# Tokens as the stationary operand: turning the products of a two-network kernel round

## The chip, the cores and the metric

The kernel runs as one program on one core of a Trainium2 chip. Its metric is device time in microseconds (us) of one execution; the time given for a kernel is the median of its runs. TensorE (PE) multiplies, VectorE (DVE), ScalarE (ACT) and GpSimd (POOL) do the work between products, and SyncE (SP) issues most loads.

## The reference, cut to what matters

The input x has 256 tokens of 1024 features. It passes through two networks of two layers each. Every layer is a feed-forward block, a mixer and a second feed-forward block, each added to the residual:

```python
def swiglu(h, w_in, w_out):
    gate, up = jnp.split(h @ w_in, 2, axis=-1)      # w_in (1024, 2 * 2816)
    return (jax.nn.silu(gate) * up) @ w_out         # w_out (2816, 1024)

def rmsnorm(x, g):
    return x * lax.rsqrt(jnp.mean(x * x, axis=-1, keepdims=True) + EPS) * g

x = x + 0.5 * swiglu(rmsnorm(x, g0), w_in0, w_out0)
x = x + mixer(rmsnorm(x, g1), ...)
x = x + 0.5 * swiglu(rmsnorm(x, g2), w_in1, w_out1)
```

The mixers are, in order: hgrn2 (`hg`: a gated linear recurrence with 8 heads, weights 1024 x 4096 and 1024 x 1024), forgetting attention (`fox`: 16 heads, the same sizes and 16 more columns), a short convolution (`conv`: 1024 x 3072 and 1024 x 1024), and a sparse attention with three branches (`nsa`), whose shared keys and values (`kv`: 1024 x 1536) are projected once from the residual ahead of the last layer. All of it is fp32.

## The kernel before

Thirteen phases run one after the other: ffn 0, hg 1, ffn 2, ffn 3, fox 4, ffn 5, ffn 6, conv 7, ffn 8, kv 9, ffn 10, nsa 11, ffn 12. The residual `x` stays on the chip with features on partitions: 8 tiles of 128 features by 256 tokens.

Each product of fp32 numbers is made of three: both operands are split into a rounded part and a rest, both in the type fp32r, and hi x hi, hi x lo and lo x hi are added in PSUM. `mm_w` multiplies with the weights stationary (128 x 128) and 256 tokens moving, and gives an output with features on partitions; `mm_x` has 128 tokens stationary and 256 weight columns moving.

```python
self.mm(out, h[:, k, s], xh[:, k], start, False, 109.0)
self.mm(out, h[:, k, s], xl[:, k], False, False, 109.0)
self.mm(out, l[:, k, s], xh[:, k], False, stop, 109.0)
```

The weights come in pieces of 1 MB, 336 in all: an `in` piece is 1024 rows by 256 columns, an `out` piece 256 rows by 1024 columns. `load` brings a piece to a raw buffer (`wr`, 4 of them), `prep` splits a quarter of it: ScalarE casts the high part `wh` (L177) and VectorE subtracts to get the low part `wl` (L179), or GpSimd does so for the quarters named in `pool_parts`. There are 4 pairs of split buffers. The order of everything is written out by hand: `self.t` counts modelled time along the products, `pump` emits a quarter of a split every `pace` ns if buffers allow, and `tick` lets background tasks (`spawn`) emit their next part when it is due. Each engine runs its own instructions in the order in which they were emitted.

A feed-forward unit (11 per block) takes a gate piece and an up piece of 256 columns: `proj` makes 2 x 16 products of three matmuls into two PSUM banks. `g1` is the gate times 1/rms, spread over partitions as `rb` (L477, VectorE), `sg` its silu (L479, ScalarE) times 1/rms again (L480, GpSimd), `av` the up half times `sg` (L484), and `ah`, `al` are its parts (L487, L488). `proj_out` multiplies the unit before with its `out` piece, 16 products, into four banks that add up over the block.

`leave` and `enter` join blocks: as a pair of output tiles is complete, VectorE adds it to `x` (L392), ScalarE and VectorE split x times the norm's gain into `xh`, `xl` (L356, L360), ScalarE squares (L370) and GpSimd adds the squares up (L372, L382). `stats` sums them over partitions with narrow matmuls (`consts,ssum`), takes the inverse root on VectorE in small steps (`rsqrt`), and `spread` puts 1/rms on all partitions with two matmuls (`dg,consts`). The first unit of a block goes through k in its outer loop, so that it can start on the first tiles of x.

In fox, kv and nsa, `nat_heads` norms heads of q and k with tokens on partitions: square (L674), sum (L675), `rsqrt`, and the factor applied as `qn` (L686), which also frees the PSUM bank; `turn` and `to_feature` transpose 128 x 128 blocks on TensorE (L250).

Of the kernel before, what the change touches and what calls it, by code (L numbers as in the profile page):

```python
# [8 lines left out]
F32 = mybir.dt.float32  # L9
# [14 lines left out]
FAR = 1e30  # L24
LEVELS = (1, 2, 4, 8, 16, 32, 64)
# [18 lines left out]
# columns of the array of per-partition vectors  # L44
# [9 lines left out]
# columns of the array of row vectors, the same on each partition  # L54
# [3 lines left out]
# columns of the array of constants  # L58
# [8 lines left out]
def positions():  # L67
    """NSA: the head at position 2 * c + half, chunk c = 4 * pair + hg."""
    return [(2 * (c // 4) + half) * 4 + c % 4 for c in range(8) for half in range(2)]


def plan(phases=PHASES):
    """The weight pieces in the order of their use: (array, index, 'in'|'out', columns or rows)."""
# [8 lines left out]

    for ph in phases:
        if ph[0] == "ffn":
            _, _, w_in, at, w_out = ph
            for u in range(NU):
                pieces.append((w_in, at, "in", block(u)))
                pieces.append((w_in, at, "in", block(NU + u)))
                if u:
                    pieces.append((w_out, at, "out", block(u - 1)))  # L90
            pieces.append((w_out, at, "out", block(NU - 1)))
        elif ph[0] == "hg":
            for p in range(4):
                pieces += [("hg_w_in", (0,), "in", block(4 * s + p)) for s in range(3)]
            pieces += [("hg_w_in", (0,), "in", block(12 + p)) for p in range(4)]
            pieces += [("hg_w_out", (0,), "out", block(p)) for p in range(4)]
        elif ph[0] == "fox":
            pieces += [("fox_w_in", (0,), "in", block(0)), ("fox_w_in", (0,), "in", block(4))]
            pieces.append(("fox_w_in", (0,), "in", range(4096, 4112)))
            pieces.append(("fox_w_in", (0,), "in", block(8)))  # L100
            for p in range(1, 4):
                pieces += [("fox_w_in", (0,), "in", block(4 * s + p)) for s in range(3)]
            pieces += [("fox_w_in", (0,), "in", block(12 + p)) for p in range(4)]
            pieces += [("fox_w_out", (0,), "out", block(p)) for p in range(4)]
        elif ph[0] == "conv":
            for p in range(4):
                pieces += [("conv_w_in_2", (0,), "in", block(4 * s + p)) for s in range(3)]
# [1472 lines left out]
```

## Time and profile before

| what | us |
|---|---|
| time, median of 3 runs (2153.5 to 2154.3) | 2153.77 |
| span of the profiled execution, first to last instruction | 2149.8 |
| busy: TensorE, weight loads, VectorE, ScalarE, GpSimd | 2097.8, 2072.7, 1409.2, 1034.0, 432.4 |
| feed-forward block 2, windows 386 to 577.6 | 191.6 |
| hg, 202.6 to 386 | 183.4 |
| fox, 768.1 to 934.2 | 166.1 |

The span is what one profiled execution shows; its own time is known only through the runs, whose median lies 4.0 us above the span, outside the first and last instruction. PE is the matmuls, whose records overlap since they are pipelined, PEld the weight loads. PEclk is the granted clock of TensorE as a share of full speed (1.00 is 2.4 GHz, 0.50 is 1.2 GHz). Each matmul record is named output<-moving,stationary. An fp32 product that is not fp32r is two instructions in the trace, a transpose is one.

### The profile page before, as it was taken

What the parts mean: (1) busy time and instruction counts of PE and PEld (TensorE: products, weight loads), DVE (VectorE), ACT (ScalarE), POOL (GpSimd) and SP (SyncE); (2) the same over time, 40 slices, a digit from 0 to 9 for tenths busy, and PEclk for the clock granted to TensorE, in tenths of its full rate; (3) what the DMA queues carried; (4) which work ended last, traced back from release to release, by engine and by line L of the source; (5) the groups of instructions that cost most, each with busy time, mean ns of one, the idle gap of its engine ahead of it and who ended that gap; (6) DMA issues with size and microseconds to landing.
All of it is one profiled execution on the core that took longest, in us unless ns stands there. A gap on an engine that the chain in (4) does not pass through costs nothing.

```text
span 2149.8 us, 41509 instructions
## 1 busy us (share of the span) xinstructions
PE 2097.8 (98%) x17273; PEld 2072.7 (96%) x17273; DVE 1409.2 (66%) x2536; ACT 1034.0 (48%) x2082; POOL 432.4 (20%) x410
## 2 busy tenths in 40 slices
PE   8999889999999997999999999999999999999999
PEld 8999889999999997999999999999999999889999
DVE  7666676755665576466567567776578665677654
ACT  5544434444454456654444444454445444665442
POOL 2002546300100026420011001110021100532000
PEclk9999999999999999999999999999999999999999
DMA  7554423595455534345545554555546555223551
GB/s 263 203 189 146 154 80 128 178 239 189 157 212 183 184 141 165 128 143 213 194 157 196 181 192 141 202 194 191 180 169 234 179 185 174 101 94 120 213 193 60
DMA packets 56701, 367.88 MB, mean 171 GB/s; under 512 B 6255, under 2 KB 10631, under 8 KB 13761
## 3 DMA queue, kind: packets, MB, share of 16 engines
q1 hardware_dynamic: 53600, 355.49, 46.2%
q0 software_dynamic: 2336, 9.02, 2.2%
q8 instruction: 135, 2.21, 0.4%
q10 hardware_dynamic: 576, 0.72, 0.1%
q14 instruction: 54, 0.43, 0.1%
HBM read 359.70 MB, written 4.46 MB: 169 GB/s over the span
## 4 chain that ended last, share of the span: by engine, by line
PE 73%; DVE 7%; ACT 2%; issue 1%; POOL 0%; DMA 0%; DVEq 0%; ACTq 0%
PE b L245 72%; DVE wl L179 2%; DVE xl L360 1%; PE b L250 1%; DVE x L392 1%; ACT wh L177 1%; DVE rs_t L423 1%; DVE rs_t L424 0%; ACT xh L356 0%; DMA cd<-cn 0%; DVE oc L1260 0%; DVE rn L425 0%; DVE nrs L425 0%; POOL ssum L372 0%; DVE nss L675 0%
## 5 line engine op out<-in xcount | busy, mean ns | idle before, releaser
L179 DVE TENSOR_TENSOR wl<-wr,wh 128x512 fp32r<-128x512 f32 x1229 | 849.6, 750 | 256.7 <-ACT wh L177 256.4
L245 PE MATMUL b<-xh,wh 128*128 128x256 f32 x3184 | 908.0, 285 | 7.0 <-ACT wh L1442 7.0
L245 PE MATMUL b<-xh,wl 128*128 128x256 f32 x3184 | 904.7, 284 | 2.5 <-DVE wl L1443 2.5
L245 PE MATMUL b<-xl,wh 128*128 128x256 f32 x3184 | 904.1, 284 | 0.0
L177 ACT CAST wh<-wr 128x512 fp32r<-128x512 f32 x1332 | 725.9, 616 | 149.9 <-issue 132.1
L245 PEld LDWEIGHTS b<-xh,wh 128*128 128x128 f32 x3184 | 613.5, 193 | 7.1 <-ACT wh L1442 7.0
L245 PEld LDWEIGHTS b<-xh,wl 128*128 128x128 f32 x3184 | 613.5, 193 | 3.4 <-DVE wl L1443 3.4
L245 PEld LDWEIGHTS b<-xl,wh 128*128 128x128 f32 x3184 | 613.6, 193 | 0.0
L245 PE MATMUL b<-ah,wh 128*128 128x256 f32 x1408 | 394.4, 280 | 0.0
L245 PE MATMUL b<-al,wh 128*128 128x256 f32 x1408 | 394.2, 280 | 0.0
L245 PE MATMUL b<-ah,wl 128*128 128x256 f32 x1408 | 394.0, 280 | 0.0
L480 POOL TENSOR_TENSOR sg<-sg,rb 128x512 f32<-128x512 f32 x88 | 114.3, 1298 | 1247.5 <-ACT sg L479 1247.5
L245 PEld LDWEIGHTS b<-al,wh 128*128 128x128 f32 x1408 | 265.1, 188 | 0.2 <-DVE al L488 0.2
L245 PEld LDWEIGHTS b<-ah,wh 128*128 128x128 f32 x1408 | 265.1, 188 | 0.0
L245 PEld LDWEIGHTS b<-ah,wl 128*128 128x128 f32 x1408 | 264.7, 188 | 0.0
L479 ACT ACTIVATE sg<-g 128x512 f32<-128x512 f32 x88 | 55.6, 632 | 320.5 <-DVE g L477 320.4
L487 ACT CAST ah<-av 128x512 fp32r<-128x512 f32 x88 | 54.6, 621 | 259.1 <-DVE av L484 259.1
L477 DVE TENSOR_TENSOR g<-b,rb 128x512 f32<-128x512 f32 x88 | 60.7, 690 | 170.9 <-PE b L245 169.0
L179 POOL TENSOR_TENSOR wl<-wr,wh 128x512 fp32r<-128x512 f32 x103 | 143.1, 1402 | 132.6 <-ACT wh L177 126.2
L245 PE MATMUL b<-wh,xh 128*128 128x256 f32 x512 | 152.7, 298 | 11.5 <-DVE qn L686 11.5
L245 PE MATMUL b<-wl,xh 128*128 128x256 f32 x512 | 146.5, 286 | 0.0
L245 PE MATMUL b<-wh,xl 128*128 128x256 f32 x512 | 146.4, 286 | 0.0
(264 smaller groups left out, 1970.9 us busy)
## 6 DMA issues: line engine op xcount, KB each, us to landing
wr<-in_W_dram SPq DMA_DIRECT2D x332, 1024.0 KB, 4.8
td<-t POOLq DMA_DIRECT2D x1, 3072.0 KB, 37.9
wr<-in_W_dram SPq DMA_DIRECT2D x8, 256.0 KB, 6.1
bc<-cd POOLq DMA_DIRECT2D x4, 512.0 KB, 5.2
w<-in_CW_dram POOLq DMA_DIRECT2D x2, 1024.0 KB, 10.3
bt<-td SPq DMA_DIRECT2D x8, 256.0 KB, 3.9
x<-in_XT_dram SPq DMA_DIRECT2D x4, 256.0 KB, 5.9
wr<-in_W_dram SPq DMA_DIRECT2D x2, 512.0 KB, 3.8
```

What stands on the lines that cost most here:

```text
L177: nc.scalar.copy(h[:, s], r[:, s])
L179: eng.tensor_tensor(l[:, s], r[:, s], h[:, s].bitcast(F32), op=ALU.subtract)
L245: self.nc.tensor.matmul(out, lhsT, rhs, start=start, stop=stop, skip_group_check=True)
L250: self.nc.tensor.transpose(out, in_, self.c("ID")[:n, :n])
L360: self.nc.vector.scalar_tensor_tensor(xs[1][:, d], self.x[:, d], g, xs[0][:, d].bitcast(F32), op0=ALU.mult, op1=ALU.subtract)
L392: nc.vector.scalar_tensor_tensor(x, acc[i], factor, x, op0=ALU.mult, op1=ALU.add)
L423: nc.vector.scalar_tensor_tensor(t, out, -1.0, out, op0=ALU.mult, op1=ALU.mult)
L477: nc.vector.tensor_tensor(g1, banks[0].rearrange("p (c t) -> p c t", c=2), self.rb2(), op=ALU.mult)
L479: nc.scalar.activation(sg, g1, AF.Silu)
L480: nc.gpsimd.tensor_tensor(sg, sg, self.rb2(), op=ALU.mult)
L487: nc.scalar.copy(ah, av)
```

## The change

The order of operands is turned in most products. Tokens (128 at a time) are stationary and weights move, 512 columns at once. This takes pieces of another shape: an `in` unit is now two half pieces, each 512 rows by 512 columns (for a feed-forward unit, 256 gate and 256 up columns side by side), `out` pieces stay as they were. `nat` makes one bank of 128 tokens by 512 columns from 8 products; `out_steps` makes the residual's increment by tokens. Only products whose result must have features on partitions (q and the forget gate of hg, all of conv, the compressed keys and values of kv, the narrow projections `mini`) keep the old order, in `feat` and `mini`.

The residual is kept by tokens, 2 tiles of 128 tokens by 1024, and `enter` turns a quarter of it (4 transposes), splits it into `xs`, and takes the sum of squares along the free axis on ScalarE. 1/rms is then a scalar per partition, so a feed-forward unit needs no `rb`: silu takes it as its scale, and `av` is one multiply with two factors. `av` has tokens on partitions and is turned (4 transposes) by the task `turn`, due 2000 ns after the unit's products, and split by `to_feature`. Only hg, conv and kv still call `spread`. The norm's gain leaves the residual's split and enters that of `in` pieces, as a scale on ScalarE and a multiply-subtract on VectorE; these pieces no longer go to GpSimd. Raw buffers are 3 instead of 4, `consts` is loaded ahead of `vec`, and input and output are laid out by tokens. In fox the ring of banks for projections has 3 banks from the start, q and k of four heads share one `nat_heads`, and `mini` and the first half of v come behind it; in kv the normed keys are made first, then `spread`, then the raw keys and values.

```diff
 def plan
+    def cols(name, at, site, idx):
+        for half in range(2):
+            pieces.append((name, at, "in", list(idx), half, site))
...
-                pieces.append((w_in, at, "in", block(u)))
-                pieces.append((w_in, at, "in", block(NU + u)))
+                cols(w_in, at, site, [*block(u), *block(NU + u)])
...
-        self.wraw = pool("wraw", 4)
+        self.wraw = pool("wraw", 3)
 def prep
-        nc.scalar.copy(h[:, s], r[:, s])
-        eng = nc.gpsimd if self.part in self.pool_parts else nc.vector
-        eng.tensor_tensor(l[:, s], r[:, s], h[:, s].bitcast(F32), op=ALU.subtract)
+        if kind == "in":
+            g = self.gain(site, 4 * half + q)
+            nc.scalar.activation(h[:, s], r[:, s], AF.Copy, scale=g)
+            nc.vector.scalar_tensor_tensor(l[:, s], r[:, s], g, h[:, s].bitcast(F32), op0=ALU.mult, op1=ALU.subtract)
+        else:
...
+            nc.scalar.copy(h[:, s], r[:, s])
+            eng = nc.gpsimd if q in self.pool_parts else nc.vector
+            eng.tensor_tensor(l[:, s], r[:, s], h[:, s].bitcast(F32), op=ALU.subtract)
...
+    def three(self, out, a, b, start, stop, cost):
+        (ah, al), (bh, bl) = a, b
+        self.mm(out, ah, bh, start, False, cost)
+        self.mm(out, ah, bl, False, False, cost)
+        self.mm(out, al, bh, False, stop, cost)
...
+    def nat_steps(self, w, j, b):
+        self.finish(*self.entering[:2 + 2 * j])
         s = slice(128 * j, 128 * j + 128)
+        for k in range(8):
+            self.three(b, self.x_of(k, s), self.rows_of(w, k), k == 0, k == 7, 216.0)
             self.tick()
+            if j and k % 4 == 3:
+                self.done()
+            yield k
...
+    def feat(self, w, half, ring=None):
+        self.finish(*self.entering)
+        b = self.bank(ring or self.P)
+        for c in range(2):
+            n = slice(256 * half + 128 * c, 256 * half + 128 * c + 128)
             for k in range(8):
+                wh, wl = self.rows_of(w, k)
+                xh, xl = self.x_of(k, slice(0, 256))
+                o = b[:, 256 * c:256 * c + 256]
+                self.mm(o, wh[:, n], xh, k == 0, False, 120.0)
+                self.mm(o, wh[:, n], xl, False, False, 120.0)
+                self.mm(o, wl[:, n], xh, False, k == 7, 120.0)
+                self.tick()
...
+    def out_steps(self, acc, first, last, z, done):
+        h, l = [p.rearrange("p (k n) -> p k n", k=2) for p in self.get()]
         self.hold = last
+        for i in range(4):
+            j, n = divmod(i, 2)
+            t, d = slice(128 * j, 128 * j + 128), slice(512 * n, 512 * n + 512)
...
             for k in range(2):
+                self.three(o, (z[:, 0, k, t], z[:, 1, k, t]), (h[:, k, d], l[:, k, d]), first and k == 0, last and k == 1, 216.0)
                 self.tick()
...
+    def enter(self, i, ring):
+        j, n = divmod(i, 2)
+        xs = self.xs
+        b = self.bank(ring)
+        for q in range(4):
+            k = 4 * n + q
+            self.transpose(b[:, 128 * q:128 * q + 128], self.x[:, j, 128 * k:128 * k + 128])
+        bb = b.rearrange("p (q t) -> p q t", q=4)
+        hi, lo = (xs[:, e, 4 * n:4 * n + 4, 128 * j:128 * j + 128] for e in range(2))
+        nc.scalar.copy(hi, bb)
+        nc.vector.tensor_tensor(lo, bb, hi.bitcast(F32), op=ALU.subtract)
+        if n:
+            sq = self.sm.tile([128, 1024], F32, name="sq", tag="sq", bufs=1)
+            nc.scalar.activation(sq, self.x[:, j], AF.Square, accum_out=self.ssq[:, j:j + 1])
         if i == 3:
+            self.stats()
+        yield 0.0
 def leave
-                self.enter(i)
+                self.entering.append(self.spawn(self.enter(i, ring), 1150.0))
...
 def ffn
+            def turn(u, av):
+                a2[u] = self.to_feature(pl, av, R, 2)
+                yield 0.0
...
+                for j in range(2):
+                    b = self.nat(w, j, I)
+                    self.finish(*self.entering)
+                    r = self.rn[:, j:j + 1]
+                    sg = pl.tile([128, 256], F32, name="sg", tag="sg")
+                    nc.scalar.activation(sg, b[:, 0:256], AF.Silu, scale=r)
+                    nc.vector.scalar_tensor_tensor(av[:, j], b[:, 256:512], r, sg, op0=ALU.mult, op1=ALU.mult)
                 if u == 1:
                     acc = [self.bank(A) for _ in range(4)]
+                before, turned = turned, self.spawn(turn(u, av), 2000.0)
                 if u:
+                    self.finish(before)
+                    self.proj_out(acc, u == 1, False, a2.pop(u - 1), None)
...
 def fox
+                heads = self.nat_heads_in_two(pl, [self.nat(w, i) for i in range(2)], "qk", pool=j > 0, bufs=3)
+                got = next(heads)
                 if j == 0:
+                    for _ in heads:
+                        pass
+                    turn = self.mini(16, X)
...
+                if j % 2 == 0:
+                    w = []
+                    v2 = pl.tile([128, 2, 512], F32, name="v", tag="v")
+                    for i in range(2):
+                        nc.scalar.activation(v2[:, i], self.nat(w, i), AF.Copy, scale=self.rn[:, i:i + 1])
...
 def kv
+            (kn,) = self.nat_heads(pl, [self.nat(w, i) for i in range(2)], "kn", bufs=1)
+            self.spread(B[2:])
+            w, raws = [], []
+            turned = []
+            for i in range(2):
+                b = self.feat(w, i)
```

## Rows read from the trace of the kernel before

**Rows 1.** The page: busy time of each engine, and the chain that ended last.

```profile
PE 2097.8 (98%) x17273; PEld 2072.7 (96%) x17273; DVE 1409.2 (66%) x2536; ACT 1034.0 (48%) x2082; POOL 432.4 (20%) x410
...
PE 73%; DVE 7%; ACT 2%; issue 1%; POOL 0%; DMA 0%; DVEq 0%; ACTq 0%
```

**Rows 2.** Windows: stretch, length, busy (instructions) by engine, PEclk, DMA share, GB/s.

```profile
202.60:386.00 183.40, 164.83 (x1307) 161.93 (x1307) 129.59 (x231) 73.81 (x168) 107.33 (x86) 0.94 0.34 117
386.00:577.60 191.60, 191.53 (x1604) 190.53 (x1603) 123.70 (x195) 89.42 (x168) 25.44 (x22) 1.00 0.65 200
768.10:934.20 166.10, 153.68 (x1228) 148.40 (x1227) 103.29 (x237) 98.79 (x226) 80.57 (x94) 0.97 0.41 146
828.00:830.00 2.00, 2.00 (x11) 2.00 (x11) 1.79 (x10) 0.94 (x4) 0.00 (x0) 0.50 1.01 377
1200.00:1300.00 100.00, 100.00 (x842) 100.00 (x842) 58.48 (x87) 44.70 (x83) 7.61 (x6) 1.00 0.53 190
```

**Rows 3.** Groups of matmuls by shape: count, busy us, mean ns, idle before.

```profile
L245 PE MATMUL b<-xh,wh 128*128 128x256 f32 x3184 | 908.0, 285 | 7.0 <-ACT wh L1442 7.0
...
L245 PE MATMUL b<-ah,wh 128*128 128x256 f32 x1408 | 394.4, 280 | 0.0
...
L245 PE MATMUL b<-wh,xh 128*128 128x256 f32 x512 | 152.7, 298 | 11.5 <-DVE qn L686 11.5
...
L245 PE MATMUL b<-zh,wh 128*128 128x256 f32 x256 | 73.2, 286 | 0.1
...
L245 PE MATMUL b<-vv,pT 128*128 128x64 f32 x192 | 22.4, 274 | 0.0
...
L245 PE MATMUL b<-dg,consts 128*128 128x128 f32 x40 | 7.5, 314 | 5.5 <-DVE dg L444 5.2
...
L245 PE MATMUL b<-consts,ssum 128*128 128x1 f32 x48 | 6.0, 230 | 0.0
...
L245 PE MATMUL b<-vcz,pcT 128*128 128x256 f32 x16 | 3.8, 379 | 0.0
```

**Rows 4.** Timeline of TensorE in fox: start us, length us, instruction.

```profile
828.20 0.41 PE L245 MATMUL b<-wh,xl 128*128 128x256 f32 x1
828.41 0.41 PE L245 MATMUL b<-wh,xh 128*128 128x256 f32 x1
```

**Rows 5.** Timeline of the weight loads (PEld) in nsa.

```profile
1873.65 1.49 PEld L245 LDWEIGHTS b<-vcz,pcT 128*128 128x128 f32 x7
1875.16 2.86 PEld L245 LDWEIGHTS b<-vv,pT 128*128 128x128 f32 x24
1877.94 0.19 PEld L245 LDWEIGHTS b<-wh,xh 128*128 128x128 f32 x1
```

**Rows 6.** Timeline of TensorE around four transposes in fox.

```profile
792.01 0.28 PE L245 MATMUL b<-wh,xl 128*128 128x256 f32 x1
792.13 0.60 PE L250 MATMUL b<-consts,qn 128*128 128x128 f32 x4
792.49 0.36 PE L245 MATMUL b<-wh,xh 128*128 128x256 f32 x1
```

**Rows 7.** Waits of TensorE: releaser, us in total, times, longest.

```profile
PE b L245 <- DVE qn L686: 11.5, 1, 11.5
...
PE b L250 <- POOL gs L608: 1.0, 3, 0.4
```

**Rows 8.** Groups of VectorE's instructions, shapes apart.

```profile
L179 DVE TENSOR_TENSOR wl<-wr,wh 128x512 fp32r<-128x512 f32 x1229 | 849.6, 750 | 256.7 <-ACT wh L177 256.4
...
L392 DVE SCALAR_TENSOR_TENSOR x<-b,x 128x512 f32<-128x512 f32 x48 | 33.2, 691 | 45.6 <-PE b L245 45.6
...
L675 DVE TENSOR_REDUCE nss<-nsq 128x8 f32<-128x512 f32 x14 | 9.6, 683 | 15.5 <-ACT nsq L674 15.5
...
L934 DVE SCALAR_TENSOR_TENSOR y<-u,vec,y 128x256 f32<-128x256 f32 x8 | 3.9, 486 | 0.3
...
L1273 DVE TENSOR_TENSOR zl<-b,zh 128x256 fp32r<-128x256 f32 x8 | 3.4, 419 | 0.5 <-ACT zh L1272 0.5
```

More of the change, by code (lines that the diff above doesn't have):

```diff
@@ L93, in plan @@
             for p in range(4):
-                pieces += [("hg_w_in", (0,), "in", block(4 * s + p)) for s in range(3)]
-            pieces += [("hg_w_in", (0,), "in", block(12 + p)) for p in range(4)]
-            pieces += [("hg_w_out", (0,), "out", block(p)) for p in range(4)]
-        elif ph[0] == "fox":
[L98 to L104, printed above, removed]
+                if p % 2 == 0:
+                    cols("hg_w_in", (0,), site, [*block(8 + p), *block(9 + p)])
@@ new lines, in plan @@
+                cols("hg_w_in", (0,), site, [*block(p), *block(4 + p)])
+            for p in range(0, 4, 2):
+                cols("hg_w_in", (0,), site, [*block(12 + p), *block(13 + p)])
+            for p in range(4):
+                rows("hg_w_out", (0,), block(p))
+        elif ph[0] == "fox":
+            for p in range(4):
+                cols("fox_w_in", (0,), site, [*block(p), *block(4 + p)])
+                if p == 0:
+                    pieces.append(("fox_w_in", (0,), "mini", list(range(4096, 4112)), 0, site))
+                if p % 2 == 0:
+                    cols("fox_w_in", (0,), site, [*block(8 + p), *block(9 + p)])
+            for p in range(0, 4, 2):
+                cols("fox_w_in", (0,), site, [*block(12 + p), *block(13 + p)])
+            for p in range(4):
+                rows("fox_w_out", (0,), block(p))
@@ L116, in plan @@
+            cols("attn_w_q_2", (0,), site, heads(2) + heads(3))
+            for j in range(4):
+                rows("attn_w_o_2", (0,), heads(j))
     return pieces
@@ L199, in pump @@
         if self.t >= self.next_prep:
[L200 removed]
+            if not self.hold and self.prep_i < self.n and self.prep_i < self.done_i + WB and self.prep_i <= self.use_i + 3:
                 self.prep()
@@ L345, in begin_site, with proj_out @@
+            yield
+        self.hold = False
+    def proj_out(self, *a):
+        for _ in self.out_steps(*a):
+            pass
     def begin_site(self, site):
-        pl = self.kvx if site == 9 and self.kvx else self.act
         self.site = site
-        self.xs = (
-            pl.tile([128, 8, 256], F32R, name="xh", tag="xh", bufs=1),
-            pl.tile([128, 8, 256], F32R, name="xl", tag="xl", bufs=1),
-        )
-        self.ssum = self.sm.tile([128, 512], F32, name="ssum", tag="ssum", bufs=1)
@@ L386, in leave @@
+    def leave(self, acc, factor, nxt, ring):
         nc = self.nc
@@ L499, in ffn @@
-            self.proj_out(acc, NU - 1, False, True, prev, done)
+            self.finish(turned)
+            done = self.leave(acc, 0.5, nxt, R)
+            self.proj_out(acc, False, True, a2.pop(NU - 1), done)
         self.P, self.aside = self.comp(A), []
@@ L1314, in nsa @@
             bias(1)
-            b0, b1 = self.proj("xx", xs, outer=True, stats=lambda: self.stats(False, R))
-            turn = self.mini(48, xs, R)
-            qs += self.nat_heads(pl, (b0, b1), ("qa", "qb"))
+            w = []
+            qs += self.nat_heads(pl, [self.nat(w, i, A) for i in range(2)], "qa", bufs=1)
+            turn = self.mini(48, R)
             self.P = A
```

555 lines of the change are left out of this document (195 added, 360 removed).

## The prediction

> **What bounds the kernel now.** I read the page first. TensorE is busy for 98% of the span and its weight loads (PEld) for 96%, and TensorE makes up 73% of the chain that ended last [rows 1]. Busy time alone proves little, since matmuls overlap, so next come the windows by stage. A feed-forward stage (386 to 577.6) keeps PE busy 191.53 of its 191.6 us at full clock, with VectorE at 123.70 and ScalarE at 89.42; only the hg stage (202.6 to 386) and the fox stage (768.1 to 934.2) leave PE idle, 18.6 and 12.4 us [rows 2]. So in most stages nothing starves TensorE, and time is the number of its instructions times their spacing.
>
> What sets the spacing? In 1200 to 1300 there are 842 matmuls in 100 us: 0.1188 us each [rows 2], 256 columns wide [rows 3]. It could be the stream of columns or the weight load. Three rows answer. In 828 to 830, after a long wait in fox, the granted clock is 0.50, the lower level (1.2 GHz) [rows 2]; matmuls of the same shape start 0.21 us apart there [rows 4], and 256 / 1.2 = 0.213: one column a clock. At 2.4 GHz that rate would give 0.107, yet 0.1188 is seen. Products only 64 wide (vv,pT) take 2.78 us for 24 loads, 0.116 each, although they stream little [rows 3, 5]. So about 0.116 is the floor that a weight load sets, and the 256-wide products sit on it. The vcz,pcT products, 256 wide in fp32, are spaced (1.49 - 0.19) / 6 = 0.217 [rows 3, 5], what 512 columns at 2.4 GHz would take (0.213): there the load is hidden.
>
> **The products.** 16,080 matmuls are 256 wide now: three times 3184 + 1408 + 512 + 256 [rows 3]. What stays so are 128 products by `feat` in hg, 192 in conv, 32 in kv and two `mini` of 8: 368, or 1104 matmuls. The other 14,976 become 7,488 that are 512 wide. Removed: 12,672 of the feed-forward blocks at 0.1188 and 2,304 others at 0.120 (the step in rows 6), 1505.4 + 276.5 = 1781.9 us. Added: 7,488 x 0.216 = 1617.4. Net -164.5 us. The trace has no 512-wide fp32r matmul; its bounds are 0.213 (the stream alone) and 0.2376 (twice today's step, if the stream and not the load takes the 0.1188). I take 0.216, since the 64-wide and the vcz rows both point to the load.
>
> The Trainium skill (TensorE: Matmul & The Clock Gate, Back-to-back issue gap) gives about 131 ns as the sustained spacing of 512-wide matmuls. By that the added products would be 7,488 x 0.131 = 981 us and the kernel near 1,407 us. This case's rows contradict it (one column a clock, 0.213 for 512), and I give it under 1 in 100.
>
> **The transposes.** The feed-forward hidden `av` now has tokens on partitions and must be turned: 8 blocks x 11 units x 4 = 352. The residual is turned as it enters a block: 12 x 16 = 192. That is 136 fours. A four that waits for nothing moves the next product from 0.12 to 0.48 us after the last one (792.01 to 792.49) [rows 6]: 0.36 each, 136 x 0.36 = +49.0 us.
>
> The Trainium skill (TensorE: Matmul & The Clock Gate, Part 4: PE-mode transpose) has about 275 ns for one transpose inside a kernel, which speaks against this change: 544 x 0.275 = 150 us. The row above, four in 0.36, decides here.
>
> **Other PE work.** The sums of the norm leave (48 narrow instructions, consts,ssum), and three of the ten spreads of 1/rms stay (28 of 40 dg,consts go) [rows 3]: 76 x 0.116 = -8.8 us. Most of PE's idle time before the spreads goes with them (5.5 us) [rows 3]; three keep theirs: -3. In all, a feed-forward unit falls from 144 x 0.1188 = 17.1 us to 72 x 0.216 + 0.36 = 15.9.
>
> **Work beside PE.** Costed at nothing in the feed-forward blocks: the g1 and POOL multiplies leave, and the gain moves into the split. A low part becomes a multiply-subtract, at 256 wide 486 ns against 419, so 512 wide some 0.82 against 0.75 [rows 8]. A unit then needs 8 x 0.82 + 4 x 0.75 + 2 x 0.49 + 0.75 = 11.3 us of VectorE beside 15.9 of PE. That is the cover; were it gone, each microsecond would count 88 times. The weights' bytes are the same: 3.1 MB in 15.9 us is 198 GB/s, and 200 was moved beside a full PE [rows 2], so one raw buffer less costs nothing either. At the start the same bytes land before the first unit is through, so the turn of x hides behind the weights still to come: 0.
>
> **Waits.**
> - fox: PE stood 11.5 us until `qn` freed a bank [rows 7], and came out of it at the lower clock [rows 2]. Now `mini` and half of `v` run ahead of that bank's next use; I leave 2: -9.
> - kv: the matmuls of the spread now come behind the whole `nat_heads` chain on VectorE (reduce 0.68, Newton steps, two qn of that width, dg), and the 96 matmuls of the first `feat` queue behind them on PE. Between 2.1 (reduce and qn alone) [rows 8] and 11.5 (the fox wait, the same helper) [rows 7]: +6.5.
> - conv: its first `feat` needs all tokens, so the last quarter's update (0.69), turn (0.36), copy and split (0.75 each) are exposed [rows 6, 8]: +2.5. After block 10 the entries share one bank, where each waits for the split before it: +3.
> - hg: input pieces no longer use POOL, so 32 parts x 0.75 = 24 us move to VectorE, busy 129.6 of 183.4 [rows 2, 8]. Between 0 and 24; VectorE has room left: +4.
> - `turn` in each unit: `av` needs a ScalarE and a VectorE step after the last matmul, while the transposes stand four products (2.6 us) later in PE's queue, ahead of the other products of `proj_out`. Between 0 and 88 x 0.33 = 29, what transposes that waited for `gs` lost [rows 7]: +10.
>
> **Sum.** -164.5 + 49.0 - 8.8 - 3 - 9 + 6.5 + 2.5 + 3 + 4 + 10 = -110.3. Span 2149.8 - 110.3 = 2039.5. The median of the runs is 4.0 above the profiled span, which gives 2043.5 us.
>
> **Rivals.**
> - *The stream is the bound, not the load.* Then 512 columns cost 0.2376 and the products save only 2.8 us, while the transposes stay: 2043.5 + 7,488 x 0.0216 = 2205, slower than before. It decides from 0.231 on. For it: 0.1188 could be 0.107 and a gap at each switch of weights. Against: 64-wide products have the same step. 8 in 100.
> - *PE waits inside each unit* (late `av`, or bursts on VectorE): 1 us x 88 less the 10 counted, 2121; from 1.4 us on it eats the gain. For it: transposes hold their place in PE's queue. Against: 2.6 us of room for two steps of 0.4 to 0.75 [rows 8]. 8 in 100, of which 2 end within 0.2% of before.
> - *Transposes do not overlap what is beside them.* A four costs the whole 0.60 of its record [rows 6]: +33, 2076, still in the range. If each of the four waited for the end of the one before, 4 x 0.274 (a narrow product's record) [rows 3] = 1.1 a four: +100, 2144. 2 in 100. The Trainium skill's rule on transposes would put it there.
> - *Every wait above at nothing*, hg and fox at PE's pace: -110.3 becomes -136, 2017. 2 in 100.
>
> **How the numbers follow.** The forecast, 2043.5, has 80 in 100. Its range: down to 2020 with the terms of turn, hg, kv and bank near their lower ends (-10, -4, -4.4, -3); up to 2085 with turn at 29, hg at 24 and kv at 11.5 (+19, +20, +5). The rivals at 2017, 2121, 2144 and 2205 lie outside and hold 20. A measurement of this kernel can tell about 0.2% (4.3 us) from no change. Faster by more: 0.80 + 0.06 + 0.02 + 0.02 = 0.90; within: 0.02; slower: 0.08.
>
> **What would show it.** Right: about 450 of the 512-wide matmuls in 100 us of a feed-forward stage, starting 0.216 apart, with gaps between their weight loads (PEld well under PE); feed-forward stages of 176 to 179 us; fours that add 0.36. Wrong: starts 0.23 or more apart, PE idle before the transposes of `av`, or VectorE near full in the feed-forward stages.

## The result, and the profile after

The changed kernel takes 2230.98 us (median of 4 runs, 2226.25 to 2231.79) against 2154.03 for the kernel before, run beside it (4 runs, 2153.5 to 2155.09): a ratio of 1.0354, interval 1.0339 to 1.0368. The forecast was 2043.5 and faster. Its profiled run took 2231.41 with a span of 2229.6, 79.8 above the span of before, where the sum said 110.3 below.

The page after: busy time and number of instructions of each engine.

```profile
PE 2115.9 (95%) x10253; PEld 1744.4 (78%) x10253; DVE 1321.4 (59%) x2502; ACT 1117.8 (50%) x2093; POOL 153.9 (7%) x187
```

Against [rows 1] TensorE has 7,020 instructions fewer and 18 us more of busy time, and 114 us in which it does nothing, where there were 52. Two things went wrong at once, then: the work didn't shrink as forecast, and TensorE waits more. The windows of the same stages (hg, feed-forward block 2, fox, and the 100 us from 1200) say where.

```profile
207.70:396.20 188.50, 166.80 (x1029) 148.56 (x1028) 133.57 (x263) 80.15 (x159) 52.06 (x48) 0.94 0.33 120
396.20:598.80 202.60, 193.98 (x863) 157.23 (x862) 111.21 (x188) 96.41 (x171) 4.72 (x5) 0.98 0.59 183
794.10:973.00 178.90, 157.33 (x759) 126.08 (x758) 103.16 (x226) 105.56 (x217) 45.65 (x65) 0.94 0.40 142
1200.00:1300.00 100.00, 100.00 (x450) 82.04 (x449) 56.88 (x90) 51.10 (x90) 0.00 (x0) 1.00 0.52 186
```

Beside [rows 2], hg is 5.1 us longer, block 2 11.0 and fox 12.8. In the last window PE is never idle, and still only 450 matmuls get through. A unit has 72 products and 4 transposes, so the forecast's 15.9 us a unit would give 478 in 100 us; at 450 a unit takes 16.9, against 17.1 before. The timeline of TensorE in one unit shows why (start, length, instruction).

```profile
1206.65 0.39 PE L280 MATMUL b<-wl,xs 128*128 128x512 f32 x1
1206.88 0.39 PE L280 MATMUL b<-wh,xs 128*128 128x512 f32 x1
1207.11 0.39 PE L280 MATMUL b<-wh,z 128*128 128x512 f32 x1
...
1209.45 0.40 PE L280 MATMUL b<-wl,z 128*128 128x512 f32 x1
1209.68 0.40 PE L280 MATMUL b<-wh,z 128*128 128x512 f32 x1
1209.92 0.60 PE L285 MATMUL b<-consts,av 128*128 128x128 f32 x4
1210.28 0.48 PE L280 MATMUL b<-wh,z 128*128 128x512 f32 x1
1210.59 0.39 PE L280 MATMUL b<-wl,z 128*128 128x512 f32 x1
```

The 512-wide products of `nat` (xs stationary) start 0.23 apart; their median step over the whole trace is 0.227. Those of `out_steps` (z stationary) step between 0.228 and 0.238: the twelve ahead of the transposes take 2.81 us (1207.11 to 1209.92), 0.2345 each, and the mean over the whole trace is 0.2336. The four transposes (L285) move the start of the next product by 0.36, from 0.24 to 0.60 after the last, as [rows 6] had it. But that product's own step is longer as well, 0.31 (1210.28 to 1210.59). Two products with the four between them take 0.91 us, and two without take 0.47: this four costs 0.44. Over the 88 fours of `av` the two products and the four take 0.90 in the median, 0.43 for the four, and from unit to unit it is 16.95 us. The groups by shape give the counts. The waits of TensorE (total, times, longest) show the second thing that went wrong.

```profile
L280 PE MATMUL b<-wh,xs 128*128 128x512 f32 x3328 | 1071.9, 396 | 7.7 <-ACT wh L202 4.4 <-DVE qn L704 2.5 <-ACT xs L407 0.8
L280 PE MATMUL b<-wl,xs 128*128 128x512 f32 x1664 | 655.7, 394 | 16.0 <-DVE wl L203 15.9
L280 PE MATMUL b<-wh,z 128*128 128x512 f32 x1664 | 567.3, 403 | 2.0 <-ACT wh L209 1.1 <-ACT gs L907 0.8 <-DVE x L1286 0.2
L280 PE MATMUL b<-wl,z 128*128 128x512 f32 x832 | 329.8, 396 | 0.5 <-DVE wl L211 0.5
```

```profile
PE b L285 <- DVE x L425: 22.6, 31, 2.1
PE b L280 <- DVE wl L203: 17.7, 14, 1.9
PE b L285 <- DVE qn L704: 14.1, 2, 9.9
...
PE b L285 <- DVE av L507: 5.6, 1, 5.6
```

The two at the top aren't in [rows 7] at all. Both come in small pieces at the joints between blocks.

### The profile page after: what moved, and what is told of

It reads as the page before. It is cut to its first block, busy times and chain, and to the rows that moved or that the text cites. A ratio compares the mean times of both kernels' runs of the same rounds, so it can differ in the third digit from the quotient of the medians.

```text
span 2229.6 us, 27195 instructions
## 1 busy us (share of the span) xinstructions
PE 2115.9 (95%) x10253; PEld 1744.4 (78%) x10253; DVE 1321.4 (59%) x2502; ACT 1117.8 (50%) x2093; POOL 153.9 (7%) x187
## 4 chain that ended last, share of the span: by engine, by line
PE 73%; DVE 8%; ACT 4%; issue 2%; DMA 1%; POOL 1%; ACTq 0%; DVEq 0%; POOLq 0%
PE b L280 70%; PE b L285 3%; DVE wl L203 2%; DVE xs L408 1%; DMA wr<-in_W_dram 1%; DVE x L425 1%; ACT xs L407 1%; ACT wh L202 1%; DVE rs_t L456 0%; DVE rs_t L455 0%; DVE oc L1254 0%; ACT sq L411 0%; DVE qn L704 0%; ACT p L1198 0%; ACT p L1209 0%
## 5 line engine op out<-in xcount | busy, mean ns | idle before, releaser
L280 PE MATMUL b<-wh,xs 128*128 128x512 f32 x3328 | 1071.9, 396 | 7.7 <-ACT wh L202 4.4
L280 PEld LDWEIGHTS b<-wh,xs 128*128 128x128 f32 x3328 | 631.5, 190 | 143.9 <-ACT wh L202 8.1
L203 DVE SCALAR_TENSOR_TENSOR wl<-wr,vec,wh 128x512 fp32r<-128x512 f32 x920 | 650.3, 758 | 105.2 <-ACT wh L202 93.3
L280 PE MATMUL b<-wl,xs 128*128 128x512 f32 x1664 | 655.7, 394 | 16.0 <-DVE wl L203 15.9
L202 ACT ACTIVATE wh<-wr,vec 128x512 fp32r<-128x512 f32 x920 | 601.1, 715 | 44.8 <-PE b L280 17.7
L280 PE MATMUL b<-wh,z 128*128 128x512 f32 x1664 | 567.3, 403 | 2.0 <-ACT wh L209 1.1
L280 PEld LDWEIGHTS b<-wl,xs 128*128 128x128 f32 x1664 | 315.6, 190 | 86.6 <-DVE wl L203 21.4
L280 PE MATMUL b<-wl,z 128*128 128x512 f32 x832 | 329.8, 396 | 0.5 <-DVE wl L211 0.5
L211 DVE TENSOR_TENSOR wl<-wr,wh 128x512 fp32r<-128x512 f32 x386 | 255.0, 705 | 23.0 <-ACT wh L209 20.9
L209 ACT CAST wh<-wr 128x512 fp32r<-128x512 f32 x420 | 236.4, 616 | 24.9 <-PE b L280 9.1
L408 DVE TENSOR_TENSOR xs<-b,xs 128x512 fp32r<-128x512 f32 x48 | 33.0, 691 | 57.4 <-ACT xs L407 57.3
```

The source lines that it names most:

```text
L202: nc.scalar.activation(h[:, s], r[:, s], AF.Copy, scale=g)
L203: nc.vector.scalar_tensor_tensor(l[:, s], r[:, s], g, h[:, s].bitcast(F32), op0=ALU.mult, op1=ALU.subtract)
L209: nc.scalar.copy(h[:, s], r[:, s])
L211: eng.tensor_tensor(l[:, s], r[:, s], h[:, s].bitcast(F32), op=ALU.subtract)
L280: self.nc.tensor.matmul(out, lhsT, rhs, start=start, stop=stop, skip_group_check=True)
L408: nc.vector.tensor_tensor(lo, bb, hi.bitcast(F32), op=ALU.subtract)
```

## The experiments

**What sets the step of a 512-wide product?** Four kernels bear on it. The first runs rows of 192 products on TensorE alone, one kind after the other:

```python
nc.tensor.matmul(b[:, 0:w], l, rhs[:, at:at + w], start=i % turn == 0, stop=i % turn == turn - 1, skip_group_check=True)
```

> The disputed cost by itself: TensorE alone runs rows of 192 matmuls, each row of one kind (nothing of the reference is computed). Theory G, a fixed gap: an fp32r matmul takes its columns at 2.4 GHz and about 13 ns more, whatever its width, so 512 wide 0.227 us, 384 wide 0.173, 256 wide 0.120, and 0.227 also with the same stationary block each time. Theory L, the prediction's: the step is the longer of the weight load (0.116) and the stream (columns / 2.4 GHz and 2.5 ns), so 512 wide 0.216, 384 wide 0.163, 256 wide 0.116 to 0.120, and the 0.227 and 0.235 of the changed kernel come from the other engines' traffic: then the row beside busy ScalarE and VectorE is slower than the one without. Theory R, a rate: 0.444 ns a column, so 0.227, 0.170, 0.114. Plain fp32, 256 wide: 0.217 in all three. Rows with another stationary tile, with the stationary block in the moving tile, or with a bank change every 6 products: the same as the first row unless the place in SBUF or the bank matters, which would account for 0.235 against 0.227.

Its timeline of TensorE, one line for each row (pa 512 wide, pb 384, pc 256, all fp32r; pg and ph plain fp32, 256 and 128 wide, two instructions each):

```profile
33.31 43.68 PE L175 MATMUL pa<-mw,st 128*128 128x512 f32 x192
76.83 33.47 PE L175 MATMUL pb<-mw,st 128*128 128x384 f32 x192
110.14 23.19 PE L175 MATMUL pc<-mw,st 128*128 128x256 f32 x192
...
263.75 83.04 PE L175 MATMUL pg<-raw,rx 128*128 128x256 f32 x384
346.63 43.04 PE L175 MATMUL ph<-raw,rx 128*128 128x128 f32 x384
```

From start to start: pb 43.52 us after pa, 0.227 a product; pc 33.31 after pb, 0.173; the next row 23.03 after pc, 0.120. Columns / 2.4 GHz are 213.3, 160.0 and 106.7 ns, so each product carries 13.3 to 13.5 ns on top, whatever its width. The same stationary tile all along, another one, the stationary operand in the moving tile, a new bank every six products: all 0.227. The load floor and the lower rate are both out. The row pk was meant to lie beside busy engines and began only after them, so it tells nothing.

Plain fp32 has no such gap: 0.216 an instruction at 256 columns, 2.5 ns above 512 clocks (two a column), and 0.1115 at 128 (the row behind ph starts at 389.43), 4.8 ns above 256 clocks. And the gap is gone at the lower clock. The changed kernel comes out of its long wait in fox at 0.50 (first window; the second is at full clock), and its 512-wide products step there as in this timeline:

```profile
852.00:854.00 2.00, 2.00 (x6) 1.53 (x5) 1.66 (x4) 2.00 (x4) 0.00 (x0) 0.50 0.00 0
856.00:858.00 2.00, 2.00 (x9) 1.49 (x8) 0.00 (x0) 0.00 (x0) 0.00 (x0) 1.00 1.02 422
```

```profile
852.08 0.63 PE L280 MATMUL b<-wl,xs 128*128 128x512 f32 x1
852.51 1.05 PE L280 MATMUL b<-wh,xs 128*128 128x512 f32 x2
853.36 0.63 PE L280 MATMUL b<-wl,xs 128*128 128x512 f32 x1
...
856.45 0.39 PE L280 MATMUL b<-wl,xs 128*128 128x512 f32 x1
856.68 0.62 PE L280 MATMUL b<-wh,xs 128*128 128x512 f32 x2
857.13 0.39 PE L280 MATMUL b<-wl,xs 128*128 128x512 f32 x1
```

Three products take 1.28 us at 1.2 GHz (0.427, exactly 512 columns) and 0.68 at 2.4 GHz (0.227). The Trainium skill (TensorE: Matmul & The Clock Gate, Back-to-back issue gap) gives columns / 1.2 GHz cold and columns / 2.4 GHz + 2.5 ns warm for an isolated gap: the lower clock agrees, and so does plain fp32 at 256 columns, counted at two clocks a column; fp32r at full clock doesn't, and the 131 ns that it calls sustained is seen nowhere.

The second kernel is the changed one with each 512-wide product made of two 256-wide halves, which undoes the width alone:

```diff
-        self.mm(out, ah, bh, start, False, cost)
-        self.mm(out, ah, bl, False, False, cost)
-        self.mm(out, al, bh, False, stop, cost)
+        parts = (slice(0, 256), slice(256, 512)) if out.shape[-1] == 512 else (slice(0, 256),)
+        for n, (l, r) in enumerate(((ah, bh), (ah, bl), (al, bh))):
+            for p in parts:
+                self.mm(out[:, p], l, r[:, p], start and n == 0 and p.start == 0, stop and n == 2, cost / len(parts))
```

> The changed kernel, with each 512-wide matmul issued as two of 256 columns with the same tokens stationary; order, pieces, turns and every other instruction as in it. The width's own worth. G: 7,488 more gaps, 2 x 0.120 against 0.227 to 0.235, so 60 to 97 us more than the changed kernel (2291 to 2328). R: 2 x 0.114 is the same, 0 us more. L with 0.227 forced by other engines: 2 x 0.120 again, 60 to 97 us more.

It took 2289.82 us (ratio to before 1.0634, 1.0618 to 1.0649), 58.8 above the changed kernel, just under the range of the gap theory. Where the products are `nat`'s it steps 0.120, as before; for `out_steps` it steps 0.1175, so two halves cost no more there than one 512-wide product (0.2345). The gain of the width is in `nat`.

What holds the output products at 0.2345? Two further kernels on TensorE alone repeat the order of `out_steps`, first beside ScalarE and VectorE, then with the operands at other places, with zeros, and beside transfers.

> TensorE alone on 512-wide fp32r products, in the two orders of the changed kernel; nothing of the reference is computed. Question: why do the products of `out_steps` step 0.231 to 0.238 us in the changed kernel where those of `nat` step 0.227. Rows: qa the order of `nat` (24 products into one bank); qb the order of `out_steps` (6 products into each of four banks, returned to in every unit); qc the same, but each bank's group begun anew; qd `nat` with ScalarE copying from another PSUM bank for some 25 us; qe `nat` with VectorE subtracting in SBUF for some 30 us; qf `out_steps` with both; qg `nat` again. Theory P (the pattern): qb steps 0.231 or more with nothing beside it, and qc tells whether returning to a bank does it (qc 0.227) or the short groups (qc 0.231). Theory N (the neighbours): qa, qb and qc all step 0.227, and qd, qe or qf rises to 0.231 to 0.238 while the other engine runs. The fixed gap found earlier (columns / 2.4 GHz + 13.5 ns) is expected of qa and qg under both: 0.227.

> TensorE alone again (nothing of the reference is computed), the order of `out_steps`, 512 wide. The run with the same pattern beside ScalarE and VectorE stepped 0.227 throughout, so neither the pattern nor those neighbours make the 0.231 to 0.238 that the changed kernel's output products take. Open: the place of the operands, their values, or transfers beside. Rows: r0x to r15x z at eight places 4 KB apart or more; sb other PSUM banks; sv the weights in other tiles, su with the two parts exchanged, sm one part from each pair; s0 z all zeros; sd with four transfers of 1 MB landing beside. Theory A (address): one or more of r..x, sb, sv, su, sm steps 0.231 or more. Theory V (values): s0 differs from r0x by 4 ns or more. Theory D (transfers): sd rises to 0.231 or more while the transfers land. If all stay at 0.227, the cause of these 7 ns (some 19 us of the whole) stays open.

Behind the warm-up every row of both stepped 0.226 to 0.227, also while ScalarE copied out of PSUM (40 copies in 24.7 us), while VectorE subtracted in SBUF (40 subtractions in 29 us) and while weights landed at 184 GB/s. So the pattern, those two neighbours, the place of z and of the weights, the banks, the values and the transfers are excluded one by one, though not all of them together, and the 7 ns, 2,496 x 0.0075 = 19 us of the whole, stay open. Two things in the traces narrow it. In the changed kernel the eight products of `nat` that follow the last of `out_steps`, with xs stationary, are slow too, 1.86 us or 0.232 each, and only the ones behind them step 0.227 again:

```profile
1213.15 0.40 PE L280 MATMUL b<-wh,xs 128*128 128x512 f32 x1
...
1215.01 0.62 PE L280 MATMUL b<-wh,xs 128*128 128x512 f32 x2
```

And the warm-up of the first of the two kernels has the slow step with no other engine and no transfer at work: from 14.71 to 16.79 us three products take 0.69 to 0.70, and 0.68 from there on. If these are the same slow step, neither z as the stationary operand nor a neighbour is needed for it.

**The joints between blocks.** VectorE's timeline at the end of block 5 of the changed kernel, and TensorE's:

```profile
1159.24 0.69 DVE L408 TENSOR_TENSOR xs<-b,xs 128x512 fp32r<-128x512 f32 x1 [1.77 <-ACT xs L407]
1159.85 0.68 DVE L425 SCALAR_TENSOR_TENSOR x<-b,x 128x512 f32<-128x512 f32 x1
1161.96 0.69 DVE L408 TENSOR_TENSOR xs<-b,xs 128x512 fp32r<-128x512 f32 x1 [1.43 <-ACT xs L407]
1162.57 0.68 DVE L425 SCALAR_TENSOR_TENSOR x<-b,x 128x512 f32<-128x512 f32 x1
```

```profile
1160.68 0.63 PE L285 MATMUL b<-consts,x 128*128 128x128 f32 x4 [0.69 <-DVE x L425]
...
1163.40 0.63 PE L285 MATMUL b<-consts,x 128*128 128x128 f32 x4 [0.70 <-DVE x L425]
```

The quarter's update of the residual (L425) starts only when the split of the quarter before it (L408) is done, since both stand in VectorE's one queue; that split waits for ScalarE's cast, the cast for the transposes, and the transposes for an update. That is a ring through three engines, 2.72 us a quarter (1159.85 to 1162.57) where the quarter's products take 1.40. The next kernel only sets the entry's due time later:

```diff
-                self.entering.append(self.spawn(self.enter(i, ring), 1150.0))
+                self.entering.append(self.spawn(self.enter(i, ring), 1350.0))
```

> The changed kernel with the entry of a quarter due 1350 ns after its update instead of 1150, so that the next quarter's update of the residual is emitted ahead of the split of the last one on VectorE. Theory Q (queue order): the update no longer stands behind a split that waits for ScalarE, three waits of 0.85 us leave at each of 11 block boundaries, -25 to -30 us. Rival: the entry ends just as late, and what leaves here returns as a wait of the next block's first products for their weights or x: -10 us or less.

2202.75 us (ratio to before 1.0226, 1.0209 to 1.0243): 28.2 less, as the theory of the queue had it. Two of its waits of TensorE, with the split of weights now on top:

```profile
PE b L280 <- DVE wl L203: 15.5, 12, 2.0
...
PE b L285 <- DVE x L425: 0.7, 1, 0.7
```

The second half piece of a block's first unit is split behind the entry's splits and the dozen steps of `stats`. The next kernel splits it earlier:

```diff
+                    if u == NU - 1:
+                        self.pace = 600.0
                     self.proj_out(acc, u == 1, False, a2.pop(u - 1), None)
...
+            self.pace = 950.0
             done = self.leave(acc, 0.5, nxt, R)
```

> The entries due 1350 ns later instead of 1150 (the version measured at 2202.75) and, in addition, the split of weights is emitted every 600 modelled ns instead of 950 beside the last but one set of output products of each feed-forward block, so that both half pieces of the next block are ready before the last set. Theory W (the low parts of the second half piece stand behind the statistics on VectorE): the waits of TensorE for wl at the block starts, 15.5 us in 12, fall to under 6 and the time by 8 to 14 us, to 2189 to 2195. Rival (the work is only moved: the same split now stands ahead of the residual updates on VectorE): the waits come back before the transposes of the residual, and the time stays within 3 us of 2203.

2189.45 us (1.0167, 1.0152 to 1.0182), 13.3 less. The wait for wl is down to 4.6 us in 6, and a feed-forward stage that waits for nothing reads:

```profile
954.40:1143.00 188.60, 188.59 (x853) 154.58 (x852) 113.24 (x188) 99.99 (x176) 0.00 (x0) 1.00 0.52 184
```

That is all the turned order is worth with PE full: 188.6 against some 190.5 before, 1.9 us a block.

**fox and kv.** The first attempt moved two chains: in kv `spread` ahead of `nat_heads`, in fox the Newton steps from GpSimd to VectorE.

> The changed kernel with the spread of kv emitted ahead of the head norms, and the Newton steps of fox on VectorE instead of GpSimd. If the 5.5 us before the spread in kv and the 10.0 and 4.4 us before the transposes of qn in fox are due to these queues: -5 in kv and -10 to -16 in fox with what the lower clock cost behind them, in all -12 to -20 us. Rival: VectorE, which is contended there, is no faster than GpSimd, and fox keeps its wait: -5 us in all.

2228.87 us (1.0353, 1.0338 to 1.0369), 2.1 less than the changed kernel: nearer to the rival's -5 than to the -12 to -20 of the theory. Its waits show that the 5.3 us for dg became a wait for wl (17.7 before the edit), and that the longest in fox shrank by 1.5 only, from 9.9:

```profile
PE b L280 <- DVE wl L203: 22.4, 16, 4.0
PE b L285 <- DVE qn L704: 11.2, 3, 8.4
```

The second attempt also speeds up the split of weights in kv, delays fox's first two `bias` tasks, and lets the split run on at the end of nsa:

```diff
-                yield 5500.0
+                yield 12500.0 if j < 2 else 5500.0
...
+            self.pace = 600.0
+            both = [self.nat(w, i) for i in range(2)]
+            self.pace = 950.0
             self.spread(B[2:])
...
-                        self.hold = j == 3
+                        self.hold = False
```

> The version measured at 2189.45 and three further orders, each in its own block: in fox the Newton steps on VectorE and the first two `bias` tasks 7 us later, so that GpSimd and VectorE are free when the first `qn` is due; in kv the spread ahead of `nat_heads` and the split of weights every 600 modelled ns beside the two products ahead of it; in nsa the split of weights not held during the last output products. Theory Q (each wait is a queue's order, and can be ordered away): fox 176.1 falls to 166 to 169, kv with block 10 239.9 to 235 to 237, nsa with block 12 322.1 to 317 to 320; in sum 2169 to 2177. Rival (the work is too much for VectorE at these places, so that a wait only changes its name, as when the kv order alone was changed): each block within 2 us of before the edit, 2184 to 2192.

2174.45 us (1.0097, 1.0080 to 1.0113), 15.0 less and inside the theory's range. kv with block 10 fell by 2.9 and nsa with block 12 by 8.0, but fox by 3.4 only, to 172.7, outside its 166 to 169. Even that is hardly clear: two versions below that leave fox as it was measure 173.3 where 176.1 stood, and 171.1 where 172.7 stood. VectorE's timeline in fox shows what is late there, and GpSimd's what goes on beside:

```profile
824.20 1.82 DVE L455 SCALAR_TENSOR_TENSOR rs_t<-nrs 128x16 f32<-128x16 f32 x1
826.05 1.19 DVE L456 TENSOR_TENSOR rs_t<-rs_t,rs_h 128x16 f32<-128x16 f32 x1
...
831.34 0.17 DVE L457 SCALAR_TENSOR_TENSOR nrs<-rs_t,nrs 128x16 f32<-128x16 f32 x1
831.55 0.18 DVE L455 SCALAR_TENSOR_TENSOR rs_t<-nrs 128x16 f32<-128x16 f32 x1
```

```profile
820.60 1.29 POOL L790 TENSOR_TENSOR bc<-bc,consts 128x512 f32<-128x512 f32 x1 [4.24 <-DMA bc<-cd]
...
829.39 1.89 POOL L795 TENSOR_TENSOR bc<-bc,ct 128x1024 f32<-128x1024 f32 x1
```

The same step takes 1.82 us while GpSimd works and 0.18 once it has stopped at 831.3. The Trainium skill (SBUF — State Buffer, Who interferes with whom) has it that an instruction of VectorE with two SBUF inputs contends with one of GpSimd that reads SBUF, and that the ports which the two share are locked for one of them at a time; the trace agrees, down to lengths (1.82 and 1.19) that are near those of GpSimd's instructions (1.03 to 1.89). Delaying `bias` in the order of emission had changed nothing, since GpSimd's queue was empty and it began when its data came.

**Buffers and a transfer.** One part of the change alone, on the kernel before: three raw buffers in place of four.

> The kernel before with one part of the change alone: three raw buffers for weights in place of four. The prediction put this at nothing. Theory T (without the fourth buffer the 3 MB transfer of `tables` delays the weights in block 2, and the weights after nsa come late): slower by 4 to 12 us, most of it in block 2 (191.6 before) and block 12 (189.8). Rival (the prediction's: a buffer less costs nothing, and the waits in block 2 of the changed kernel belong to its two half pieces per unit): within 2 us of before.

2160.25 us (1.0031, 1.0020 to 1.0043): 7 us, the size that the theory named, but not in its place. Block 2 stayed at 191.7; nsa went from 124.4 to 130.0 and the first block from 202.6 to 204.4. In nsa the granted clock is lower too (0.93 against 0.97), so how much of the 5.6 is late weights isn't settled. A fourth buffer in the changed kernel wasn't tried.

In the changed kernel block 2 is 11.0 us longer. ScalarE waits there for weights while `tables` writes 3 MB: 21.9 us in five waits, against 11.1 in two before.

> As the run with the earlier split, and the one transfer of 3 MB that `tables` writes during feed-forward block 2 is issued in eight parts, 9 us of modelled time apart. Theory T (that transfer delays the weights' own, and three raw buffers can't cover it): the two waits of block 2 at some 450 and 458 us (2.8 and 4.75) fall below 2 in sum, the block from 203 us to 195 to 198, and the time falls by 4 to 7 us against the run without it. Rival (what is late there is ScalarE's queue or the weights' order, not the transfer): block 2 stays at 202 to 204 and the time within 2 us.

2191.80 us (1.0180, 1.0163 to 1.0197), 2.3 more: with the transfer in eight parts of two partitions each its queue moved 5760 packets in block 2 in place of 832, and the block grew to 207.6, above the numbers of both theories (195 to 198, and 202 to 204). So the run left the question open. Next the transfer was moved whole, with the rest of `tables`:

```diff
-                if i == min(2, len(ph) - 1):
+                if i == 0:
...
-        yield 1500.0
+        yield 150000.0
         nc.gpsimd.dma_start(self.td, t1[:, None, :].to_broadcast([16, 128, 384]))
```

> The version measured at 2174.45, and the 3 MB transfer of `tables` goes out at the start of hg in place of the middle of feed-forward block 2; its small matmuls come in block 0. In hg the weights leave more of the DMA engines free (0.34 busy before, against 0.65 in block 2). Issuing the transfer in eight parts, tried before, made 5760 packets of it in place of 832 and block 2 slower, so that run didn't tell whether the transfer is the cause. Theory T (the transfer makes ScalarE wait for weights in block 2): block 2 falls from 203.1 to 189 to 191 us, hg stays within 2 us of 182.5, the sum is 2160 to 2164. Rival (the wait belongs to block 2's own weights): block 2 stays above 200, the sum within 3 us of 2174.

2179.67 us (1.0125, 1.0109 to 1.0142), 5.2 more, for two opposite reasons. The windows of hg and of block 2 with the transfer at the start of hg:

```profile
206.80:407.70 200.90, 166.65 (x1029) 149.05 (x1028) 130.98 (x260) 78.43 (x157) 57.70 (x52) 0.91 0.44 123
407.70:596.30 188.60, 188.60 (x854) 154.59 (x852) 113.02 (x188) 98.68 (x175) 0.00 (x0) 1.00 0.52 184
```

Block 2 is at 188.6 with PE never idle, and hg, where the transfer now runs, paid 18.4 for it: the transfer was the cause, with the small instructions of `tables` that moved along.

**A version with all of it.** The transfer goes out 40 us of modelled time later, where hg's own transfers fall to 110 and then 53 GB/s (in 266 to 286 and 286 to 306 of the version at 2174.45, against 163 in hg's first 20 us), and fox's Newton steps run on GpSimd ahead of `bias` in its queue.

```diff
-        yield 150000.0
+        yield 190000.0
...
-                yield 12500.0 if j < 2 else 5500.0
+                yield 16000.0 if j < 2 else 5500.0
...
-                heads = self.nat_heads_in_two(pl, [self.nat(w, i) for i in range(2)], "qk", bufs=3)
+                heads = self.nat_heads_in_two(pl, [self.nat(w, i) for i in range(2)], "qk", pool=j > 0, bufs=3)
```

> The version measured at 2174.45 with two orders mended by what the last two runs showed. (1) The 3 MB transfer of `tables` freed block 2 (188.6 in place of 203.1) but at the start of hg it made hg 18.4 us longer; it now goes out some 50 us into hg, where the transfers of weights nearly stop. (2) In fox VectorE's steps on 128 x 16 took 0.84 to 1.82 us each while GpSimd worked on `bias` and 0.17 to 0.18 once it was done; the Newton steps now run on GpSimd and ahead of `bias` in its queue. Theory: block 2 188 to 190, hg 182 to 185, fox from 172.7 to 166 to 169; in sum 2153 to 2162, near the kernel before (2153.4). Rival for (1): wherever the transfer goes, it takes its price: hg above 190 and the sum above 2166. Rival for (2): the wait for `qn` is that of its whole chain, fox stays above 171. And if the forecast's order of things held for products, such a version would have to lie well below before, at 2050 to 2070; with the products as measured it can't pass below about 2130, where every wait is gone.

2162.77 us (5 runs; 1.0041, 1.0028 to 1.0055), just above the range given. The longest wait for `qn` in fox is down from 10.2 to 4.4 us. The page's engines, and the windows of hg, block 2 and fox:

```profile
PE 2093.9 (97%) x10253; PEld 1737.2 (80%) x10253; DVE 1327.6 (61%) x2502; ACT 1119.0 (52%) x2093; POOL 156.0 (7%) x187
```

```profile
207.90:392.30 184.40, 163.71 (x1030) 146.47 (x1028) 132.61 (x260) 78.29 (x157) 56.11 (x52) 0.95 0.47 134
392.30:580.90 188.60, 188.60 (x854) 154.59 (x852) 113.02 (x187) 98.68 (x175) 0.00 (x0) 1.00 0.51 184
769.50:938.10 168.60, 154.46 (x759) 125.01 (x758) 103.33 (x220) 101.99 (x212) 48.66 (x67) 0.97 0.37 138
```

Orders alone took 68.2 us off the changed kernel. It still doesn't beat the one before; no version here does. The 2130 of that expectation is the kernel before less the 23 us by which products, transposes and other PE work shrink at 0.36 a four, and the waits of before are still in it; at 0.43 a four it comes to 2140.

## Why the prediction was wrong, step by step

**The products** are the step that failed first: "I take 0.216, since the 64-wide and the vcz rows both point to the load." 4,992 products at 0.227 and 2,496 at 0.2345 make 1718.5 us, so the term is 1718.5 - 1781.9 = -63.4 in place of -164.5. Each row that it leaned on stood for something else. The vcz products are plain fp32, which has no gap of this size (pg). The step at the lower clock is one column a clock because fp32r has no gap there either. The 64-wide products are plain fp32 too (`pT` and `vv` are F32 tiles), so their 0.116 says nothing of an fp32r load; plain fp32 at 128 columns, alone on TensorE, steps 0.1115 (ph). The 256-wide products at 0.120 are 106.7 + 13.3, close to 0.116 by chance. The rival "The stream is the bound, not the load" had the mechanism in half a sentence, "0.107 and a gap at each switch of weights", though the gap doesn't need a switch (the row with one stationary tile has it). Its price was wrong: two of today's steps is the upper end, 0.2376, and a gap paid once a product lies between. The mean, 1718.5 / 7,488 = 0.2295, is below the 0.231 from which that rival was to decide, and by this term alone the kernel would have come to 2043.5 + 101.1 = 2144.6, still a little faster than before.

**The transposes** were sized too small: 136 fours at 0.43 are 58.5 us in place of 49.0. The prediction read the cost off [rows 6], which end one product too early; the next line of that view has the rest.

```profile
792.69 0.28 PE L245 MATMUL b<-wl,xh 128*128 128x256 f32 x1
```

From 792.01 to 792.69 two products and four transposes take 0.68 us. Two products alone take 0.24, so the four cost 0.44 there as well: 0.08 of it shows only in the step behind the next product's start, 0.20 in place of 0.12. With the 9.5 us more the forecast comes to 2154.1, which is the time of before: these two terms alone take the whole gain away.

**The waits** made it slower. Products, transposes and the other PE work sum to -63.4 + 58.5 - 8.8 = -13.7, near the 1.9 us that each of the eight feed-forward blocks saves where nothing waits. The span grew by 79.8, so 93 us are waits and what comes with them. TensorE's idle time is 62 of these (114 against 52); up to 19 more are the lower clock, an estimate from the mean granted clocks of 0.983 and 0.991 and the two spans. The prediction's list came to +14. Missing from it, with what the runs give for each: the entry's ring at the joints, 28.2; the second half piece behind `stats`, 13.3. The sentence "Costed at nothing in the feed-forward blocks" had asked whether VectorE had time enough (56.9 us of 100, it had), and not in what order its queue would hold the work. "One raw buffer less costs nothing either" fell too: 7 us in the old order. The transfer of `tables`, 188.6 against 203.1 in block 2, 14.5, wasn't seen at all.

**The smaller terms.** `turn`: +10 forecast; `av` is waited for once, 5.6 us, in block 2 where the weights were late, so nothing by itself. kv: +6.5, measured 5.3 before dg; right, though kv and block 10 together grew by 11.4 (245.0 against 233.6). fox: -9 forecast, +12.8 measured. The wait for `qn` stayed (9.9 against 11.5), since more than the bank that frees late was behind it: GpSimd's `bias` stood ahead of the Newton steps. With that order mended fox came down from 176.1 to 168.6 in the end, of which some 2 to 3 us also came and went without an edit there. hg: +4, measured 5.1, part of it the joint. conv: +2.5, measured 104.9 against 93.0, of which 6 went with the two edits at the joints (98.8). Some 24 of the 93 us are left in the last version, against 14 forecast: the first block (207.9 against 202.6), conv (100.4 against 93.0) and fox (168.6 against 166.1) are still longer than before. That rest wasn't taken apart further.

**What would have shown it.** "Starts 0.23 or more apart" was named as the sign of failure and is what `out_steps` shows; VectorE near full was named too and didn't come.

## What to carry to other kernels

Before a product is made twice as wide, find what its step is made of in the very data type and at the very clock in question: a gap of 13.5 ns of 120 is all that doubling the width can halve, and transposes that the turned order needs can eat it (here less than 0.2 of a unit's 17 us was left). Read the cost of what is put between two products up to the second product behind it. A step put "beside" a full engine is free only if its place in its own queue is free: ask of each queue what stands ahead of the step that the next transfer or transpose waits for, above all where one block hands over to the next. And an engine with an empty queue can't be held back by emitting its work later in the order; give it other work first, or make the work depend on something.

## What the runs showed of the hardware that was not expected

- fp32r products: columns / 2.4 GHz + 13.3 to 13.5 ns at 256, 384 and 512 columns, with or without a change of the stationary tile; no gap at 1.2 GHz (0.427 at 512). Plain fp32: 2.5 ns at 256 columns, 4.8 at 128.
- Output products in the kernel: 0.1175 at 256 wide and 0.2345 at 512, against 0.120 and 0.227 for `nat`; alone on TensorE the same pattern steps 0.227. The eight `nat` products behind them have the slow step too (0.232). Unexplained.
- Four 128 x 128 transposes between products cost 0.43 to 0.44 us; 0.08 of it lies in the step of the product behind them (0.31 in place of 0.2345, 0.20 in place of 0.12).
- Steps of VectorE on 128 x 16: 0.84 to 1.82 us beside GpSimd, 0.17 to 0.18 without.
- Cutting a transfer of 3 MB out of 16 partitions into eight of 2 raised the packets of its queue in block 2 from 832 to 5760.
